# Loading and squaring the second row tile first, in a fixed order of the first norms, with norm weights on 97 rows

## The chip, the cores and the metric

The kernel runs on one core of a Trainium2 chip. A core has TensorE (PE, matrix multiply; its weight loads are listed as PEld), VectorE (DVE), ScalarE (ACT), GpSimd (POOL) and SyncE (SP), which run side by side, each through its own queue in order, and 16 DMA engines that serve all queues. The metric is the time of one execution on the device in microseconds. The kernel before took 877.15 us, the median of three runs (876.75, 877.15, 880.12).

## The reference, cut to what matters

The program is one encoder layer on 512 rows (tokens) of width 1024 in float32: an RMS norm, a product with `w_in`, two parallel mixers (a state-space scan and a gated chunk mixer), a gated merge, cross-attention to a memory of 256 rows, and a gated feed-forward part.

```python
def rms_norm(x, g):
    xf = x.astype(jnp.float32)
    y = xf * lax.rsqrt(jnp.mean(xf * xf, axis=-1, keepdims=True) + EPS)
    return (y * g.astype(jnp.float32)).astype(x.dtype)
...
        n = rms_norm(h, mix_norm_g[i])
        proj = n @ w_in[i]
        xa = proj[..., :OFF_U]
        zu = proj[..., OFF_U:OFF_V]
        zv = proj[..., OFF_V:OFF_GA]
```

Only the first norm and the first product, the first 512 columns of `zv`, are touched by the change.

## The kernel before

Rows are worked in four tiles of 128 (`xt[:, t, :]`, t = 0 to 3; x0 to x3 below). A float32 product is made of three products of a faster type: each operand is split into a high part, which ACT casts, and a low part, which DVE gets by subtraction (`split`, L85 and L86); `mm3` (L358) multiplies high by high, high by low and low by high. So each k tile of 128 costs three matmuls, and each weight block costs a cast and a subtraction before its first use.

Weights come in blocks of 512 KB in an order laid down in `plan`. A block is loaded by SP (`load_raw`, L137), split (`split_w`) and used (`next_w`); `raw`, `hi` and `lo` have three buffers each. The first product is a token product (`tokm`, L399): a bank of PSUM per row tile, four weight blocks of two k tiles each (w0 to w3), each used for the four row tiles. `tok_block` does one row tile with one or more blocks. One row tile with one block is six matmuls, the whole first product 96.

The start, before the first product, is in `first_rows` (L575) and the loop behind it (L598):

- Six idle matmuls (`idles`) go to PE, on a tile `idle` of the auxiliary PSUM pool (three buffers); the product banks are five.
- SP loads the norm's weights as one row (`g_row`), the first half of x0, w0, x1, w1, x2, w2, x3. ACT's queue loads the second half of x0. Two matmuls with a one-row operand (L579) spread `g_row` over 128 partitions into PSUM (`pg`).
- `row_sums` (L502) squares each half of a row tile on ACT with a running sum. `rms_factor` (L490) adds the two sums and scales them on DVE (L495, L496) and takes the power -0.5 on POOL (L497). Two DVE instructions scale the halves by that factor and by the norm's weights (L583 for x0, straight out of `pg`; L512 for the others, from the copy `g_mix`, made by ACT).
- `to_feat` (L514) transposes four 128x128 pieces on PE into an auxiliary bank (L520) and splits them into `xn_hi` and `xn_lo`.

All instructions are put in order, engine by engine, by a planner that simulates the program with its own costs. `in_order` pins an instruction behind the one traced just before it on its engine; while `pinned[0]` is true, `split` and `sum_sq` pin theirs. Behind the start, a side program (`s5_setup`, L620) prepares the scan: it loads small parameters, exponentiates the step sizes (L672, on ACT) and is spread between the products by `tick`.

Of the kernel before, what the change touches and what calls it, by code (L numbers as in the profile page):

```python
# [9 lines left out]
F32 = mybir.dt.float32  # L10
F32R = mybir.dt.float32r
AF = mybir.ActivationFunctionType
ALU = mybir.AluOpType
# [4 lines left out]
P = 128  # L18
D = 1024
T = 512  # L20
NT = T // P
KD = D // P
M = 256
NM = M // P
EPS = 1e-6
# [10 lines left out]
OFF_V = OFF_U + GW  # L36
# [16 lines left out]
def hybrid_layer_kernel(  # L53
# [8 lines left out]
    nc = tc.nc  # L62
    x, mem, out = x[0], mem[0], out[0]
    w_in, w_glu, w_proj_a, w_proj_b, w_out = w_in[0], s5_w_glu[0], w_proj_a[0], w_proj_b[0], w_out[0]
# [6 lines left out]
    np_ = ctx.enter_context(tc.tile_pool(name="norm", bufs=2))  # L71
# [5 lines left out]
    def bank(name):  # L77
        return pm.tile([P, 512], F32, tag="mm", name=name)

    def aux(name, shape=(P, 512)):  # L80
        return pa.tile(list(shape), F32, tag="aux", name=name)

    def split(dst_hi, dst_lo, src):

        hi = nc.scalar.copy(dst_hi, src)  # L85
        lo = nc.vector.tensor_tensor(dst_lo, src, dst_hi.bitcast(F32), ALU.subtract)  # L86
        if pinned[0]:
            in_order(hi)
            in_order(lo)


    pinned = [False]
    in_order = tc.keep_in_program_order
# [5 lines left out]
    plan, tiles = [], []  # L99
# [60 lines left out]
    stp = [None]  # L160
# [169 lines left out]
    def next_w(*key):  # L330
        i = used_w[0]
        used_w[0] += 1
        assert len(plan[i][0]) == len(key) and plan[i][0][1:] == key[1:] and plan[i][0][0] is key[0]
        for j in range(i, min(i + FAR + 1, len(plan))):
            begin(j, i)
            if j - 1 >= len(tiles) and j - 1 <= i + SPLITS:
                split_w(j - 1)
        for j in range(len(tiles), min(i + SPLITS + 1, len(plan))):
            split_w(j)
        tile_, tiles[i] = tiles[i], None  # L340
        return tile_
# [7 lines left out]
    def load_raw(j):  # L349
        begin(j, j)  # L350

    def split_w(j):
        tiles.append(plan[j][2]())
# [45 lines left out]
    def tokm(w, c0, act, nk, evac, ntok=NT, last=2, kpt=2, hooks={}, cut=None, t0=0):  # L399


        toks = range(t0, t0 + ntok)
        ps = {t: bank(f"pt{t - t0}") for t in toks}
        nw = nk // kpt
        held = []
        full = slice(0, 512)
        for wi in range(nw):
            hi, lo = next_w(w, wi * kpt, kpt, c0, 512)
            held.append((wi, hi, lo))
            if wi in hooks:  # L410
                hooks[wi]()
            if wi < nw - last:
                todo, held = held, []
                for t in toks:
                    end = cut is not None and t == ntok - 1 and wi == nw - last - 1
                    tok_block(ps[t], t, todo, act, kpt, full, wi == 0, end)
                    if end:
                        cut(None, ps[t])
                tick(1.3 * ntok)
        for t in toks:  # L420
            if cut is not None and t == ntok - 1:
                for i in range(2):
                    p = aux("pcut", (P, 256))
                    tok_block(p, t, held, act, kpt, slice(256 * i, 256 * i + 256), True, True)
                    cut(i, p)
            else:
                tok_block(ps[t], t, held, act, kpt, full, nw == last, True)
                evac(t, ps[t])
            tick(1.3 * len(held))

    def tok_block(ps, t, ws, act, kpt, cs, first, final):
        tsl = slice(t * P, (t + 1) * P)
        for i, (wi, hi, lo) in enumerate(ws):
            for k in range(kpt):
                kk = wi * kpt + k
                mm3(ps, (act[0](kk, tsl), act[1](kk, tsl)) if callable(act[0]) else
                    (act[0][:, kk, tsl], act[1][:, kk, tsl]),
                    (hi[:, k, cs], lo[:, k, cs]), first and i == k == 0,
                    final and i == len(ws) - 1 and k == kpt - 1)

    side = {"gen": None, "credit": 0.0, "rate": 0.0, "now": 0, "later": []}

# [47 lines left out]
    def rms_factor(ss, r=None):  # L490

        ms = np_.tile([P, 1], F32, tag="ms", name="ms", bufs=2)
        if r is None:
            r = np_.tile([P, 1], F32, tag="r", name="r", bufs=2)
        nc.vector.tensor_tensor(ms, ss[:, 0:1], ss[:, 1:2], ALU.add)  # L495
        nc.vector.tensor_scalar(ms, ms, 1.0 / D, EPS, ALU.mult, ALU.add)  # L496
        nc.gpsimd.tensor_tensor(r, ms, mhalf, ALU.pow)  # L497
        return r

    HALF = (slice(0, 512), slice(512, 1024))  # L500

    def row_sums(src):  # L502
        ss = np_.tile([P, 2], F32, tag="ss", name="ss", bufs=2)
        for i in range(2):
            sum_sq(ss[:, i:i + 1], src[:, HALF[i]])
        return ss

# [3 lines left out]
        for i in range(2):  # L511
            nc.vector.scalar_tensor_tensor(dst[:, HALF[i]], src[:, HALF[i]], r, g[:, HALF[i]], ALU.mult, ALU.mult)  # L512

    def to_feat(src, hi, lo, tsl, full=None, skip=None, part=(0, 1)):  # L514

        for q in part:
            ps = aux("ptr", (P, 4, P))
            for j in range(4):
                k = 4 * q + j
                nc.tensor.transpose(ps[:, j, :], src[:, k * P:(k + 1) * P], ident)  # L520
            if q != skip:
                split(hi[:, 4 * q:4 * q + 4, tsl], lo[:, 4 * q:4 * q + 4, tsl], ps)
            if full is not None:
                nc.scalar.copy(full[:, 4 * q:4 * q + 4, tsl], ps)
# [19 lines left out]
    def token_slot(name, place=NEAR):  # L544
        return tuple(slot(tag, (P, KD, T), F32R, name, place) for tag in "BC")
# [3 lines left out]
    s5p = s5.enter_context(tc.tile_pool(name="s5", bufs=1))  # L549


    idle = aux("idle", (P, P))

    def idles(n):
        for i in range(n):
            in_order(nc.tensor.matmul(idle, ones, ones, start=True, stop=True))
# [2 lines left out]
    warm = np_.tile([P, 1], F32, tag="ms", name="warm", bufs=2)  # L559
    nc.scalar.activation(warm, mhalf, AF.Square)  # L560


    g_mix = np_.tile([P, D], F32, tag="gain", name="g_mix", bufs=2)
    g_row = np_.tile([1, D], F32, tag="gain", name="g_row", bufs=2)
    nc.sync.dma_start(g_row, mix_norm_g)
    xt = slot("A", (P, NT, D), F32, "xt")
    nc.sync.dma_start(xt[:, 0, HALF[0]], x[0:P, HALF[0]])
    nc.scalar.dma_start(xt[:, 0, HALF[1]], x[0:P, HALF[1]])
    for t in range(1, NT):
        load_raw(t - 1)  # L570
        nc.sync.dma_start(xt[:, t, :], x[t * P:(t + 1) * P])
    xn_hi, xn_lo = token_slot("xn")
    xn = (xn_hi, xn_lo)

    def first_rows():  # L575

        pg = [aux("pg") for i in range(2)]
        for i in range(2):
            in_order(nc.tensor.matmul(pg[i], ones[0:1, :], g_row[:, HALF[i]], start=True, stop=True))  # L579
        r = rms_factor(row_sums(xt[:, 0, :]))  # L580
        in_order(nc.scalar.copy(g_mix[:, HALF[0]], pg[0]))
        for i in range(2):
            in_order(nc.vector.scalar_tensor_tensor(xt[:, 0, HALF[i]], xt[:, 0, HALF[i]], r, pg[i], ALU.mult, ALU.mult))  # L583
        raw = plan[0][3].pop("raw")
        hi = wp.tile([P, 2, 512], F32R, tag="hi", name="whi", bufs=3)
        lo = wp.tile([P, 2, 512], F32R, tag="lo", name="wlo", bufs=3)
        pinned[0] = True
        for q in range(2):
            split(hi[:, q, :], lo[:, q, :], raw[:, q, :])
            if q == 0:  # L590
                in_order(nc.scalar.copy(g_mix[:, HALF[1]], pg[1]))
            to_feat(xt[:, 0, :], xn_hi, xn_lo, slice(0, P), part=(q,))
        tiles.append((hi, lo))

    first_rows()
    split_w(1)
    ss = row_sums(xt[:, 1, :])
    for t in range(1, NT):  # L598
        rms_scale(xt[:, t, :], g_mix, xt[:, t, :], ss)
        if t == 1:  # L600
            ss = row_sums(xt[:, 2, :])
        to_feat(xt[:, t, :], xn_hi, xn_lo, slice(t * P, (t + 1) * P))
        if t == 1:
            ss3 = row_sums(xt[:, 3, :])
            pinned[0] = False
        if t == 2:
            ss = ss3

    ud = dp.tile([SW, Q, NCH], F32, name="ud")
    yd = [dp.tile([GO * C, Q, NCH], F32, name=f"yd{o}") for o in range(NO)]
# [4 lines left out]
    def s5_setup():  # L620
# [4 lines left out]
        def small():  # L625
            used[0] += 1
            return slab[:, used[0] - 1, :]

        ls = small()
        for d in range(2):  # L630
            nc.sync.dma_start(ls[64 * d:64 * d + 64, :], s5_log_step[0, d].partition_broadcast(64))
        lam = []
        lrows = s5p.tile([G, 2, 2, 64], F32, tag="etmp", name="lrows")
        for i, src in enumerate((s5_lam_re, s5_lam_im)):
# [33 lines left out]
        st["c"] = (cr, ci)  # L668


        stp, a, rho, th, n, sn, hs, cs = (small() for _ in range(8))
        A_.activation(stp, ls, AF.Exp)  # L672
        V.tensor_tensor(a, lr, stp, ALU.mult)
        A_.activation(rho, a, AF.Exp)
        V.tensor_tensor(th, li, stp, ALU.mult)
# [343 lines left out]
    def zv_evac(half):  # L1019
        def f(t, ps):  # L1020
            nc.scalar.activation(zt[:, t, half * 512:(half + 1) * 512], ps, AF.Gelu_apprx_tanh,
                                 accum_out=zsum[:, t, half:half + 1])
        return f
# [2 lines left out]
    wsr, wst = wsx[:, 0], wsx[:, 1]  # L1026
    side["gen"] = s5_program()
    side["rate"] = RATE
    tokm(w_in, OFF_V, xn, KD, zv_evac(0))

    u = s5p.tile([P, G, NCH], F32, tag="u", name="u")

# [503 lines left out]
    held = []  # L1536
# [324 lines left out]
```

## Time and profile before

| | us |
|---|---|
| median of three runs | 877.15 |
| profiled execution | 876.45 |
| its span, first to last instruction | 874.7 |
| PE busy | 862.7 (99%) |
| DVE busy | 660.7 (76%) |
| ACT busy | 464.3 (53%) |
| first product matmul starts | 9.64 |
| first matmul of the next product starts | 41.77 |

The span is shorter than the time by what lies before the first and after the last instruction. The page gives busy time by engine, the chain of work that ended last and the costliest groups; the timeline gives instructions in order of time with what ended the idle time before them. An arrow `out<-in` names the tile written and the tiles read.

### The profile page before, as it was taken

The numbers are of one execution on the slowest core, as the hardware profiler recorded it, in microseconds if no ns is written. First come the engines' busy times: TensorE is split into PE (matmuls) and PEld (weight loads), VectorE is DVE, ScalarE is ACT, GpSimd is POOL, SyncE is SP. The second block draws the span as 40 slices with busy tenths as digits, with TensorE's granted clock in tenths as the row PEclk, the third lists the DMA queues.
The fourth block names the chain that finished last, engine by engine and source line by source line (L and its number), as shares of the span: only waits on it lengthen the run. The fifth ranks groups of instructions, "written<-read, shape, count | busy, mean of one in ns | idle before, by whom it ended". The sixth has DMA issues, their size and how long they took to land.

```text
span 874.7 us, 14741 instructions
## 1 busy us (share of the span) xinstructions
PE 862.7 (99%) x5766; PEld 767.7 (88%) x5766; DVE 660.7 (76%) x1072; ACT 464.3 (53%) x693; POOL 85.1 (10%) x115
## 2 busy tenths in 40 slices
PE   9999999999999999999999999999999999999997
PEld 6788888888889988889899878999999999988875
DVE  6699885999846768568757746767877768899875
ACT  5644953244255543447546535545555555656664
POOL 1002201211020001100001001001111111000010
PEclk9999999999999999999999999999999999999999
DMA  8769565888663898735688655547899998366673
GB/s 254 198 191 291 112 174 147 194 228 202 157 196 95 275 319 236 255 95 168 196 244 247 157 135 154 145 144 174 214 243 229 209 234 218 97 191 206 193 230 106
DMA packets 116488, 169.56 MB, mean 194 GB/s; under 512 B 9265, under 2 KB 81473, under 8 KB 116290
## 3 DMA queue, kind: packets, MB, share of 16 engines
q1 hardware_dynamic: 96450, 140.59, 50.2%
q0 software_dynamic: 19680, 27.50, 20.1%
q8 instruction: 45, 0.74, 0.3%
q10 hardware_dynamic: 288, 0.52, 0.2%
q14 instruction: 25, 0.20, 0.1%
HBM read 159.71 MB, written 48.73 MB: 238 GB/s over the span
## 4 chain that ended last, share of the span: by engine, by line
PE 90%; DMA 4%; DVE 3%; ACT 2%; issue 1%; SPq 1%; DVEq 0%; ACTq 0%
PE pf L358 26%; PE pt L358 17%; PE px L1156 12%; PE pq L1156 6%; PE dx L358 5%; PE dq L358 3%; PE pv L1156 3%; PE qx L1156 2%; PE dv L358 2%; PE pz L890 2%; DMA e<-ed 1%; PE psc L358 1%; PE qq L1156 1%; PE ptr L520 1%; PE po L358 1%; DMA slab<-in_s_log_step_dram 1%
## 5 line engine op out<-in xcount | busy, mean ns | idle before, releaser
L85 ACT CAST whi<-wraw 128x1024 fp32r<-128x1024 f32 (+1 forms) x145 | 148.4, 1025 | 158.1 <-PE pf L358 54.8
L86 DVE TENSOR_TENSOR wlo<-wraw,whi 128x1024 fp32r<-128x1024 f32 (+1 forms) x145 | 172.0, 1189 | 66.8 <-ACT whi L85 66.1
L358 PE MATMUL pf<-xn,whi 128*128 128x512 f32 x448 | 140.3, 393 | 0.0
L358 PEld LDWEIGHTS pf<-xn,whi 128*128 128x128 f32 x448 | 83.7, 188 | 17.4 <-issue 0.4
L358 PE MATMUL pf<-xn,wlo 128*128 128x512 f32 x224 | 87.6, 392 | 0.0
L1156 PE MATMUL px<-fn,whi 128*128 128x256 f32 x480 | 83.3, 276 | 0.0
L1156 PEld LDWEIGHTS px<-fn,whi 128*128 128x128 f32 x480 | 72.5, 188 | 0.2
L86 DVE TENSOR_TENSOR wlo<-b,whi 128x1024 fp32r<-128x1024 f32 x40 | 48.9, 1223 | 27.4 <-ACT whi L85 27.4
L85 ACT CAST whi<-b 128x1024 fp32r<-128x1024 f32 x40 | 42.2, 1054 | 50.7 <-PE px L1156 27.8
L1156 PE MATMUL px<-fn,wlo 128*128 128x256 f32 x240 | 66.4, 277 | 0.0
L1156 PE MATMUL pq<-s,whi 128*128 128x256 f32 x320 | 55.0, 276 | 0.0
L358 PE MATMUL dx<-whi,s 128*128 128x512 f32 x166 | 52.2, 391 | 0.8 <-DVE h L1785 0.8
L86 DVE TENSOR_TENSOR wlo<-t,whi 128x1024 fp32r<-128x1024 f32 x30 | 36.8, 1225 | 19.5 <-ACT whi L85 19.5
L85 ACT CAST whi<-t 128x1024 fp32r<-128x1024 f32 x30 | 31.6, 1054 | 35.3 <-PE pv L1156 12.4
L358 PEld LDWEIGHTS pf<-xn,wlo 128*128 128x128 f32 x224 | 42.1, 188 | 8.8 <-issue 0.2
L1156 PEld LDWEIGHTS pq<-s,whi 128*128 128x128 f32 x320 | 48.2, 188 | 0.0
L1156 PEld LDWEIGHTS px<-fn,wlo 128*128 128x128 f32 x240 | 45.1, 188 | 0.0
L358 PE MATMUL pt<-whi,xn 128*128 128x512 f32 x128 | 44.2, 413 | 0.6 <-ACT xn L85 0.6
L1156 PE MATMUL pq<-s,wlo 128*128 128x256 f32 x160 | 44.2, 276 | 0.0
L358 PEld LDWEIGHTS dx<-whi,s 128*128 128x128 f32 x166 | 31.1, 188 | 7.8 <-issue 1.2
L358 PE MATMUL dx<-wlo,s 128*128 128x512 f32 x83 | 32.3, 391 | 0.0
L1156 PEld LDWEIGHTS pq<-s,wlo 128*128 128x128 f32 x160 | 30.1, 188 | 0.0
(454 smaller groups left out, 2195.0 us busy)
## 6 DMA issues: line engine op xcount, KB each, us to landing
wraw<-in_w_in_dram SPq DMA_DIRECT2D x36, 512.0 KB, 4.9
dsum<-in_w_down_dram SPq DMA_DIRECT2D x20, 512.0 KB, 6.2
wraw<-dsum SPq DMA_DIRECT2D x20, 512.0 KB, 3.9
b<-in_w_gate_dram SPq DMA_DIRECT2D x15, 512.0 KB, 5.2
b<-in_w_up_dram SPq DMA_DIRECT2D x15, 512.0 KB, 5.7
wraw<-in_w_down_dram SPq DMA_DIRECT2D x15, 512.0 KB, 4.7
dsum<-in_w_down_dram POOLq DMA_DIRECT2D x10, 512.0 KB, 7.7
dsum<-dsum POOLq DMA_DIRECT2D x10, 512.0 KB, 8.2
```

What stands on the lines that cost most here:

```text
L85: hi = nc.scalar.copy(dst_hi, src)
L86: lo = nc.vector.tensor_tensor(dst_lo, src, dst_hi.bitcast(F32), ALU.subtract)
L358: m = nc.tensor.matmul(ps, a[x], b[y], start=start and i == 0, stop=stop and i == 2, skip_group_check=free)
L520: nc.tensor.transpose(ps[:, j, :], src[:, k * P:(k + 1) * P], ident)
L890: nc.tensor.matmul(ps[:, g, :], wt[:, g, :], u[:, o * GO + g, :], start=True, stop=True)
L1156: nc.tensor.matmul(ps[:, j, :], a[x], b[y], start=start and j == k == i == 0, stop=k == 3 and i == 2, skip_group_check=True)
```

## The change

- SP's order of loads becomes `g_row`, first half of x0, x1, w0, w1, x2, w2, x3.
- `g_row` has 97 partitions: DVE clears rows 0 to 95, the weights are loaded into row 96, and the two spreading matmuls take 97 rows of ones and of `g_row`.
- The second half of x0 is squared before the first half.
- The whole of `first_rows` is pinned on PE, ACT and DVE. Both first row tiles are squared before anything of the first product. The second half of `g_mix` is copied by DVE, not by ACT. Three idle matmuls stand between the transposes of x0's first half and the first product. The product itself begins inside `first_rows`: the blocks (row tile, weight block) come as (0,0), (0,1), (1,0), (1,1), with the transposes and scalings of x0 and x1 in between. Six matmuls of a block are pinned too (`turn`).
- `tokm` is not used for the first product: row tiles 2 and 3 follow with w0 and w1, then all four with w2 and w3.
- The Exp of the step sizes is traced at the head of `s5_setup` and pinned on ACT.
- `idle` lies in a bank of the product pool.

```diff
-    def row_sums(src):
+    def row_sums(src, halves_=(0, 1)):
         ss = np_.tile([P, 2], F32, tag="ss", name="ss", bufs=2)
-        for i in range(2):
+        for i in halves_:
             sum_sq(ss[:, i:i + 1], src[:, HALF[i]])
...
-    idle = aux("idle", (P, P))
+    idle = bank("idle")[:, :P]
...
+    G_ROW = 96
     g_mix = np_.tile([P, D], F32, tag="gain", name="g_mix", bufs=2)
-    g_row = np_.tile([1, D], F32, tag="gain", name="g_row", bufs=2)
-    nc.sync.dma_start(g_row, mix_norm_g)
+    g_row = np_.tile([P, D], F32, tag="gain", name="g_row", bufs=2)
+    nc.vector.memset(g_row[0:G_ROW], 0.0)
+    nc.sync.dma_start(g_row[G_ROW:G_ROW + 1], mix_norm_g)
...
     for t in range(1, NT):
-        load_raw(t - 1)
         nc.sync.dma_start(xt[:, t, :], x[t * P:(t + 1) * P])
+        for i in ((0, 1), (2,), ())[t - 1]:
+            load_raw(i)
...
+    def row_feat(t, q):
+        to_feat(xt[:, t, :], xn_hi, xn_lo, slice(t * P, (t + 1) * P), part=(q,), turned=True)
+
+    def row_scale(t, i, r, g):
+        in_order(nc.vector.scalar_tensor_tensor(xt[:, t, HALF[i]], xt[:, t, HALF[i]], r, g, ALU.mult, ALU.mult))
+
     def first_rows():
-
         pg = [aux("pg") for i in range(2)]
         for i in range(2):
-            in_order(nc.tensor.matmul(pg[i], ones[0:1, :], g_row[:, HALF[i]], start=True, stop=True))
-        r = rms_factor(row_sums(xt[:, 0, :]))
+            in_order(nc.tensor.matmul(pg[i], ones[0:G_ROW + 1, :], g_row[0:G_ROW + 1, HALF[i]], start=True, stop=True))
+        pinned[0] = True
+        ss = row_sums(xt[:, 0, :], (1, 0))
+        r = rms_factor(ss)
         in_order(nc.scalar.copy(g_mix[:, HALF[0]], pg[0]))
         for i in range(2):
-            in_order(nc.vector.scalar_tensor_tensor(xt[:, 0, HALF[i]], xt[:, 0, HALF[i]], r, pg[i], ALU.mult, ALU.mult))
+            row_scale(0, i, r, pg[i])
+        in_order(nc.vector.tensor_copy(g_mix[:, HALF[1]], pg[1]))
+        r = rms_factor(row_sums(xt[:, 1, :]))
+        row_feat(0, 0)
+        idles(3)
         raw = plan[0][3].pop("raw")
         hi = wp.tile([P, 2, 512], F32R, tag="hi", name="whi", bufs=3)
         lo = wp.tile([P, 2, 512], F32R, tag="lo", name="wlo", bufs=3)
-        pinned[0] = True
-        for q in range(2):
-            split(hi[:, q, :], lo[:, q, :], raw[:, q, :])
-            if q == 0:
-                in_order(nc.scalar.copy(g_mix[:, HALF[1]], pg[1]))
-            to_feat(xt[:, 0, :], xn_hi, xn_lo, slice(0, P), part=(q,))
+        for k in range(2):
+            split(hi[:, k, :], lo[:, k, :], raw[:, k, :])
+            if k == 0:
+                row_scale(1, 0, r, g_mix[:, HALF[0]])
         tiles.append((hi, lo))
+        first_product(0, 0)
+        row_feat(1, 0)
+        split_w(1)
+        row_scale(1, 1, r, g_mix[:, HALF[1]])
+        first_product(0, 1)
+        ss = row_sums(xt[:, 2, :])
+        row_feat(0, 1)
+        first_product(1, 0)
+        first_product(1, 1)
+        row_feat(1, 1)
+        pinned[0] = False
+        return ss
...
+    def first_product(t, wi, turn=True):
+        tok_block(pt[t], t, [(wi,) + tiles[wi]], xn, 2, slice(0, 512), wi == 0, False, turn)
+
+    ss = first_rows()
+    for t in range(2, NT):
         rms_scale(xt[:, t, :], g_mix, xt[:, t, :], ss)
-        if t == 1:
-            ss = row_sums(xt[:, 2, :])
+        if t == 2:
+            ss = row_sums(xt[:, 3, :])
         to_feat(xt[:, t, :], xn_hi, xn_lo, slice(t * P, (t + 1) * P))
...
+        stp = small()
+        in_order(A_.activation(stp, ls, AF.Exp))
...
-    tokm(w_in, OFF_V, xn, KD, zv_evac(0))
+    evac = zv_evac(0)
+    for wi in range(2):
+        held = tiles[wi]
+        next_w(w_in, wi * 2, 2, OFF_V, 512)
+        tiles[wi] = held
+        for t in range(2, NT):
+            first_product(t, wi, False)
+        tiles[wi] = None
+        tick(5.2)
+    held = [(wi,) + next_w(w_in, wi * 2, 2, OFF_V, 512) for wi in (2, 3)]
+    for t in range(NT):
+        tok_block(pt[t], t, held, xn, 2, slice(0, 512), False, True)
+        evac(t, pt[t])
+        tick(2.6)
```

More of the change, by code (lines that the diff above doesn't have):

```diff
@@ L429, in tokm, with tok_block @@
             tick(1.3 * len(held))
-    def tok_block(ps, t, ws, act, kpt, cs, first, final):
+    def tok_block(ps, t, ws, act, kpt, cs, first, final, turn=False):
         tsl = slice(t * P, (t + 1) * P)
@@ L438, in tok_block @@
                     (hi[:, k, cs], lo[:, k, cs]), first and i == k == 0,
-                    final and i == len(ws) - 1 and k == kpt - 1)
+                    final and i == len(ws) - 1 and k == kpt - 1, turn=turn)
     side = {"gen": None, "credit": 0.0, "rate": 0.0, "now": 0, "later": []}
@@ L494, in rms_factor @@
             r = np_.tile([P, 1], F32, tag="r", name="r", bufs=2)
-        nc.vector.tensor_tensor(ms, ss[:, 0:1], ss[:, 1:2], ALU.add)
-        nc.vector.tensor_scalar(ms, ms, 1.0 / D, EPS, ALU.mult, ALU.add)
+        fixed = in_order if pinned[0] else lambda i: i
+        fixed(nc.vector.tensor_tensor(ms, ss[:, 0:1], ss[:, 1:2], ALU.add))
+        fixed(nc.vector.tensor_scalar(ms, ms, 1.0 / D, EPS, ALU.mult, ALU.add))
         nc.gpsimd.tensor_tensor(r, ms, mhalf, ALU.pow)
@@ L512, in rms_scale, with to_feat @@
             nc.vector.scalar_tensor_tensor(dst[:, HALF[i]], src[:, HALF[i]], r, g[:, HALF[i]], ALU.mult, ALU.mult)
-    def to_feat(src, hi, lo, tsl, full=None, skip=None, part=(0, 1)):
+    def to_feat(src, hi, lo, tsl, full=None, skip=None, part=(0, 1), turned=False):
         for q in part:
@@ L519, in to_feat @@
                 k = 4 * q + j
-                nc.tensor.transpose(ps[:, j, :], src[:, k * P:(k + 1) * P], ident)
+                m = nc.tensor.transpose(ps[:, j, :], src[:, k * P:(k + 1) * P], ident)
+                if turned:
+                    in_order(m)
             if q != skip:
@@ L586, in first_rows @@
         lo = wp.tile([P, 2, 512], F32R, tag="lo", name="wlo", bufs=3)
-        pinned[0] = True
-        for q in range(2):
-            split(hi[:, q, :], lo[:, q, :], raw[:, q, :])
-            if q == 0:
-                in_order(nc.scalar.copy(g_mix[:, HALF[1]], pg[1]))
-            to_feat(xt[:, 0, :], xn_hi, xn_lo, slice(0, P), part=(q,))
-        tiles.append((hi, lo))
[L595 to L598, printed above, removed]
+        for k in range(2):
+            split(hi[:, k, :], lo[:, k, :], raw[:, k, :])
+            if k == 0:
+                row_scale(1, 0, r, g_mix[:, HALF[0]])
+        tiles.append((hi, lo))
+        first_product(0, 0)
[10 more added lines that the diff above has]
+        return ss
+    pt = {t: bank(f"pt{t}") for t in range(NT)}
+    def first_product(t, wi, turn=True):
+        tok_block(pt[t], t, [(wi,) + tiles[wi]], xn, 2, slice(0, 512), wi == 0, False, turn)
+    ss = first_rows()
+    for t in range(2, NT):
         rms_scale(xt[:, t, :], g_mix, xt[:, t, :], ss)
-        if t == 1:
-            ss = row_sums(xt[:, 2, :])
+        if t == 2:
+            ss = row_sums(xt[:, 3, :])
         to_feat(xt[:, t, :], xn_hi, xn_lo, slice(t * P, (t + 1) * P))
[L603 to L607, printed above, removed]
     ud = dp.tile([SW, Q, NCH], F32, name="ud")
@@ L668, in s5_setup @@
         st["c"] = (cr, ci)
-        stp, a, rho, th, n, sn, hs, cs = (small() for _ in range(8))
-        A_.activation(stp, ls, AF.Exp)
+        a, rho, th, n, sn, hs, cs = (small() for _ in range(7))
         V.tensor_tensor(a, lr, stp, ALU.mult)
```

## The prediction

> **What bounds the kernel now.** I read the page's busy table first, then the chain that ended last, then the timeline of the first 42 us, because the diff touches nothing that runs later. The page:
>
> ```profile
> span 874.7 us, 14741 instructions
> ...
> PE 862.7 (99%) x5766; PEld 767.7 (88%) x5766; DVE 660.7 (76%) x1072; ACT 464.3 (53%) x693; POOL 85.1 (10%) x115
> ...
> PE 90%; DMA 4%; DVE 3%; ACT 2%; issue 1%; SPq 1%; DVEq 0%; ACTq 0%
> ```
>
> PE is busy for 99% of the span and carries 90% of the chain. Whatever the change does, the later 830 us are bound by PE, whose work there stays the same: an edit to the start moves the end by as much as it moves the moment at which PE has a given amount of work behind it. So I need the start, instruction by instruction (columns of the timeline: start, length, engine, line, operation, and in brackets the idle time before it with what ended it).
>
> ```profile
> 1.06 2.93 PE L556 MATMUL idle<-ones 128*128 128x128 f32 x12 [1.06 <-DVE mhalf L481]
> 1.56 0.43 SPq L137 DMA_DIRECT2D wraw<-in_w_in_dram  x1
> 2.03 0.47 SPq L571 DMA_DIRECT2D xt<-in_x_dram  x1
> 3.92 3.78 PE L579 MATMUL pg<-g_row,ones 1*128 1x512 f32 x4
> 4.50 0.63 ACT L486 ACTIVATE sq<-xt 128x512 f32<-128x512 f32 x1 [1.84 <-DMA xt<-in_x_dram]
> 5.58 1.20 SPq L631 DMA_DIRECT2D slab<-in_s_log_step_dram  x2
> 5.65 0.19 ACT L486 ACTIVATION_READ_ACCUMULATOR sq<-xt 128x1 f32 x1
> 5.87 0.16 DVE L495 TENSOR_TENSOR ms<-ss 128x1 f32<-128x1 f32 x1 [3.68 <-ACT sq L486]
> 6.30 0.57 POOL L497 TENSOR_TENSOR r<-ms,mhalf 128x1 f32<-128x1 f32 x1 [4.53 <-DVE ms L496]
> 6.90 1.58 DVE L583 SCALAR_TENSOR_TENSOR xt<-xt,r,pg 128x512 f32<-128x512 f32 x2 [0.68 <-POOL r L497]
> 7.58 0.62 ACT L85 CAST whi<-wraw 128x512 fp32r<-128x512 f32 x1 [0.97 <-DMA wraw<-in_w_in_dram]
> 7.79 1.94 PE L520 MATMUL ptr<-ident,xt 128*128 128x128 f32 x8
> 8.40 0.68 DVE L86 TENSOR_TENSOR wlo<-wraw,whi 128x512 fp32r<-128x512 f32 x1
> 9.64 0.80 PE L358 MATMUL pt<-whi,xn 128*128 128x512 f32 x1
> 10.24 0.63 PE L358 MATMUL pt<-wlo,xn 128*128 128x512 f32 x1
> 10.47 1.07 ACT L85 CAST whi<-wraw 128x1024 fp32r<-128x1024 f32 x1
> 10.66 1.06 PE L358 MATMUL pt<-whi,xn 128*128 128x512 f32 x2
> 11.58 1.22 DVE L86 TENSOR_TENSOR wlo<-wraw,whi 128x1024 fp32r<-128x1024 f32 x1
> 13.33 0.63 PE L358 MATMUL pt<-whi,xn 128*128 128x512 f32 x2
> 13.79 0.40 PE L358 MATMUL pt<-wlo,xn 128*128 128x512 f32 x1
> 14.62 1.38 PE L520 MATMUL ptr<-ident,xt 128*128 128x128 f32 x8
> 15.83 0.23 ACT L672 ACTIVATE slab<-slab 128x32 f32<-128x32 f32 x1 [0.68 <-DMA slab<-in_s_log_step_dram]
> 16.59 0.50 PE L358 MATMUL pt<-whi,xn 128*128 128x512 f32 x1 [0.58 <-ACT xn L85]
> 20.35 0.62 PE L358 MATMUL pt<-whi,xn 128*128 128x512 f32 x2
> 20.80 0.39 PE L358 MATMUL pt<-wlo,xn 128*128 128x512 f32 x1
> 21.03 0.62 PE L358 MATMUL pt<-whi,xn 128*128 128x512 f32 x2
> 21.94 1.47 PE L520 MATMUL ptr<-ident,xt 128*128 128x128 f32 x12
> 28.25 0.19 DVE L673 TENSOR_TENSOR slab<-slab 128x32 f32<-128x32 f32 x1
> 41.77 0.62 PE L358 MATMUL pf<-xn,whi 128*128 128x512 f32 x2
> ```
>
> See two things. At 10.24 to 10.66 one product matmul takes 0.42 us from start to start; from 20.35 to 21.03 three take 0.68, or 0.227 each. At 13.33 to 13.79 two take 0.46: PE ran at half speed until about 13. And PE has a hole around 16: the Exp of L672 stood in front of the x cast on ACT and waited 0.68 us for a small load.
>
> ```profile
> 9.62:21.93 12.31, 10.35 (x36) 1.00 1.02 259
> 21.93:41.76 19.83, 15.60 (x61) 1.00 0.72 200
> ```
>
> These rows (stretches of time, PE on tile pt alone: length, busy, number of matmuls; one falls into both) are my yardstick: by 21.94 PE has 36 product matmuls and 16 transposes behind it. 36 x 0.227 = 8.2 us, and the 8 transposes of row tile 1 at about 0.11 us (12 in 1.47 with the last one's tail) another 0.9. Of 12.3 us some 3.2 were lost to the slow clock and to holes. This is all that a better start can win from 9.64 on. After 21.94 PE is busy throughout.
>
> **The change, part by part.** *Loads.* x1 and w0 change places on SP's queue, one issue slot of about 0.45 us (1.56 to 2.03); nothing else on SP or on ACT's queue moves. In the trace the first half-megabyte behind x0 (w0) was there at 7.58, when the cast that waited for it started, and x1, issued second at 2.03, landed 6.8 us later; x0's second half, on ACT's queue from its start at about 0.75, took 3.1 (columns: size, us from issue to landing):
>
> ```profile
> xt<-in_x_dram SPq DMA_DIRECT2D x1, 512.0 KB, 6.8
> xt<-in_x_dram ACTq DMA_DIRECT2D x1, 256.0 KB, 3.1
> ```
>
> So I give the first place's 7.5 to x1 and the second's 8.85 to w0; w1, x2, w2 and x3 keep their places. g_row goes to row 96 while DVE clears rows 0 to 95. The memset is priced by that of `ones`: 128 columns cost 165 ns, so 1,024 cost at most 8 times that, 1.3 us:
>
> ```profile
> L479 DVE MEMSET ones<- 128x128 f32 x1 | 0.2, 165 | 0.8 <-PEq L1847 0.8
> L955 DVE COPY yn<-py 128x512 f32<-128x512 f32 x4 | 2.8, 692 | 10.3 <-PE pyt L961 10.3
> ```
>
> DVE is idle then (its 3.68 us before 5.87), so I take nothing for it. If g_row's load waited for the memset, SP's queue behind it would slip from 0.75 to about 2.4 us, by some 1.6; that is the upper end.
>
> *Gain matmuls and clock.* The two fp32 gain matmuls have 512 columns before and after, so their work is the same; only the rows change, 1 to 97. No row here shows 97. What rows show: PE was busy without a break from 1.06 to 9.6 and was still at half speed at 10.24; of that, 3.92 to 7.7 were one-row matmuls. The full-height products from 9.64 on had it at full speed some 3.5 to 4 us later. Nearest to 97 rows is 128, so I take it that they count, and that PE is at full speed from somewhere between 4.5 and 8 us. [...]
>
> *First norms.* The half that ACT's queue loads is squared first, so ACT starts at about 3.9 and has both halves by 5.25, not 5.84. The same steps follow: sum and scale on DVE, the power on POOL (0.57), r at 6.3; the first scaling 6.3 to 7.05, the second by 7.8. The copy of the gains' second half goes from ACT to DVE: 0.69 us by the L955 row, so DVE is free at 8.4 to 9.0. ACT copies the first half and then stands waiting for x1: its two squares take 7.55 to 8.9 (1.34 for the pair, 4.50 to 5.84). r of row tile 1 is there at 9.9.
>
> *The fixed order, and what it costs.* On ACT the cast of x0's first transposes (eight took 1.94 at half speed, so four are ready at 8.8, or 7.6 at full speed) is queued behind the squares of x1: 8.9 to 9.5. Then w0's two halves, 9.5 to 10.1 and to 10.75. On DVE the order is x0's low part to 10.2, w0's first low half to 10.9, the scaling of x1 (0.75) to 11.65, w0's second low half to 12.3. So PE, with three idle matmuls covered (six took 2.93 at half speed, so three are 1.5 at most, from 7.6 or 8.8 on, while ACT squares x1 and casts; without that cover they cost their 0.7 to 1.5), begins its first product at 10.15, but its fifth matmul needs the second low half: block (0,0) ends at 12.8 and not before. Only then come x1's four transposes, to 13.3; only then, on ACT, their cast, 13.45 to 14.05; only behind that w1's cast (1.07) to 15.1; w1's low part on DVE (1.22) to 16.35. Block (0,1) gets its second matmul at 16.35 and ends at 17.5. From there PE is dense: four transposes to 17.95, two blocks of six (2.7 us) to 20.7, four transposes to 21.1.
>
> At 21.1 PE then has 24 products and 16 transposes. The yardstick has 36: 12 x 0.227 = 2.7 us more, so the new kernel reaches the same state at 23.8, against 21.94: 1.9 us late.
>
> *Steps at no cost.* Exp leaves the middle of ACT's queue and stands behind the last x cast, near 25 us by my sum: its result is first used at 28.25, and the 0.68 us wait goes; the sum above holds it already, since the new wait on w1's cast is later still. The squares of x2 and w2's split fall in ACT's time after 15.1, while PE works from 16.35 on. The idle tile takes a product bank instead of an auxiliary one; four token banks and it fill the five. The new order over tokens and weights in the first product moves 96 matmuls about but adds none. The small gain left out: with PE later, x2 and x3 are less likely to keep it waiting; I take 0.2 us.
>
> Sum: +1.9 - 0.2 = +1.7. The profiled execution took 876.45 (span 874.7 and 1.75 around it), 0.7 below the median of 877.15. So 876.45 + 1.7 = 878.1, 1.0 above the median, or 0.1%. A measurement of this kernel can hardly tell 0.5% (4.4 us) from no change.
>
> **Rivals.** *The clock stays low (slower).* If 97 rows do not count, products cost 0.42 until PE has been dense for 3.5 us. By the same chain the first block ends at 13.2, w1's low part at 17.15, block (0,1) at 19.3; the clock rises at about 20.5, the 24th product and the transposes end at 23.3: 2.2 us more, 880.3. If the clock rises only at 24, the twelve products and eight transposes from 19.3 on cost up to 2.6 more, 882. It decides against 881.5 when dense work must last about 4.5 us from 17.15. For it: PE is half empty from 8 to 16. Against it: the clock held through the thin stretch at 14.65 to 16.6 and fell only after the last matmul, and PE's longest hole in my forecast is 1.8 us:
>
> ```profile
> 868.23 0.28 PE L358 MATMUL pcut<-whi,s 128*128 128x256 f32 x1
> 872.00:874.70 2.70, 0.00 (x0) 0.75 0.46 175
> ```
>
> Three quarters of the clock on the mean over the last 2.7 us: it fell about 5 us after the last matmul. Chance 0.22, over half of that still within 0.5%.
>
> *The order is kinder than I count (slightly faster).* If x1 lands at 6.5 and DVE gets w0's second low half before PE needs it, PE is dense from about 12.3: four products left of the first twelve plus the next twelve with their transposes end at 18.2, against 19.2 for the same state before (21.94 - 2.7): 1.0 us gained, 875.4. For it: no row shows x1 in the first place; against it: each engine's queue in the diff keeps its order, so w1's cast cannot pass x1's. Chance 0.25. A gain over 0.5% needs 872.8; the 3.2 us lost in the yardstick stretch are the ceiling (873.2), and w0 lands later, so 0.02.
>
> *SP's queue waits for the memset.* +1.6 on the whole chain: 879.7. Against it: the two loads of L631 write two row ranges of one tile, and the second was issued by 6.78, long before anything of them had landed (near 15.8, where Exp's wait ended). Chance 0.08.
>
> **How the numbers follow.** Forecast 0.45, low clock 0.22, kinder order 0.25, memset 0.08. Range: down to 874.8, the 875.4 of the kinder order with 0.6 for the early landing of x1; up to 881.6, between the two ends of the low clock. Within 0.5% (872.8 to 881.5): 0.87; slower 0.11; faster 0.02.
>
> **What would show it.** After's timeline: ACT's squares of x1 waiting for its load until about 7.5; transposes of x0 at about 0.11 us each if the clock is up by 8; w1's cast starting behind x1's cast near 14; a PE hole before it, and the product blocks dense from 16.4; no DMA wait of ACT before Exp. The first feature product (L358, pf, at 41.77 before) should start near 43.5. Wrong would be: w1 cast before 12, PE dense by 13, or product matmuls at 0.42 after 16.

## The result and the profile after

The changed kernel takes 881.5 us (median of six runs, 880.98 to 882.23), the kernel before 876.95 in the six runs beside it: a ratio of 1.0050, 95% interval 1.0037 to 1.0064. In a second comparison (E5 below) it took 880.3 against 877.2, ratio 1.0037 (1.0023 to 1.0051). It is slower, by 0.4 to 0.5%.

The page of the kernel after:

```profile
span 879.6 us, 14755 instructions
...
PE 861.7 (98%) x5772; PEld 768.2 (87%) x5772; DVE 662.0 (75%) x1074; ACT 463.7 (53%) x692; POOL 86.1 (10%) x115
...
PEclk8999999999999999999999999999999999999999
```

The span is 4.9 us longer and PE is busy 1.0 us less: PE waits more, and most of that in the first slice. The clock row reads 8 there and 9 on the page before, but the rows do not compare directly: the page counts the clock as full up to its first recorded change, which came at 4.12 us here and only at 13.19 before. The timeline of the start of the kernel after (start, length, engine, line, operation, idle time before it and what ended it) against the rows of the prediction:

```profile
0.75 0.35 SPq L569 DMA_DIRECT2D g_row<-in_mix_norm_g_dram  x1
1.18 0.91 DVE L568 MEMSET g_row<- 96x1024 f32 x1 [0.16 <-issue]
3.39 0.63 ACT L486 ACTIVATE sq<-xt 128x512 f32<-128x512 f32 x1 [0.73 <-DMA xt<-in_x_dram]
7.62 0.63 ACT L486 ACTIVATE sq<-xt 128x512 f32<-128x512 f32 x1 [2.02 <-DMA xt<-in_x_dram]
8.86 0.56 ACT L85 CAST xn<-ptr 128x512 fp32r<-128x512 f32 x1
9.99 0.51 PE L358 MATMUL pt<-whi,xn 128*128 128x512 f32 x1 [1.94 <-ACT whi L85]
13.08 1.05 PE L521 MATMUL ptr<-ident,xt 128*128 128x128 f32 x4
14.17 0.58 ACT L85 CAST xn<-ptr 128x512 fp32r<-128x512 f32 x1 [3.71 <-PE ptr L521]
14.65 1.05 ACT L85 CAST whi<-wraw 128x1024 fp32r<-128x1024 f32 x1
15.76 0.50 PE L358 MATMUL pt<-whi,xn 128*128 128x512 f32 x1 [1.62 <-ACT whi L85]
17.02 0.50 PE L358 MATMUL pt<-wlo,xn 128*128 128x512 f32 x1 [0.77 <-DVE wlo L86]
17.77 0.23 ACT L652 ACTIVATE slab<-slab 128x32 f32<-128x32 f32 x1
18.69 1.06 PE L521 MATMUL ptr<-ident,xt 128*128 128x128 f32 x4
23.05 1.03 PE L521 MATMUL ptr<-ident,xt 128*128 128x128 f32 x8
45.77 0.62 PE L358 MATMUL pf<-xn,whi 128*128 128x512 f32 x2
```

ACT stands idle for 3.71 us before the cast of x1 at 14.17, although w1 has been loaded since about 10.2 (issued near 2.5, landed 7.7 us later); PE then has no work from 14.1 to 15.76 and next to none to 17.02. The first feature product starts at 45.77 instead of 41.77. The windows of PE alone in the kernel after, in steps of the 3.41 us that lie between two of its changes of clock, 10.95 and 14.36 (stretch, length, busy, number of matmuls, granted clock):

```profile
4.12:7.53 3.41, 2.53 (x11) 1.00 0.84 273
7.53:10.95 3.42, 1.18 (x7) 1.00 1.04 407
10.95:14.36 3.41, 3.19 (x9) 0.50 0.97 308
14.36:17.77 3.41, 1.25 (x4) 1.00 1.02 161
17.77:21.19 3.42, 3.42 (x11) 0.50 1.05 223
```

The clock is up from 4.12, falls at 10.95, rises at 14.36, falls at 17.77 just as the work becomes dense, and is up from 21.19 to 877.93, near the end of the span. In the 3.42 us before the first fall PE was busy for 1.18 us, in the 3.41 before the second for 1.25. So 4.0 us are lost by 45.8. A further 1.0 comes where PE waits for small loads of the scan's outputs. The waits of PE between 240 and 280 us (us in total, times, longest), first after, then before:

```profile
PE py L966 <- DMA e<-ed: 1.8, 1, 1.8
PE py L966 <- DMA tt<-kd: 1.0, 3, 0.4
```

```profile
PE py L946 <- DMA e<-ed: 1.2, 1, 1.2
PE py L946 <- DMA tt<-kd: 0.6, 2, 0.3
```

### The profile page after: what moved, and what is told of

Its sections match the earlier page's. It is cut to its first block, busy times and chain, and to the rows that moved or that the text cites. A ratio compares the mean times of both kernels' runs of the same rounds, so it can differ in the third digit from the quotient of the medians.

```text
span 879.6 us, 14755 instructions
## 1 busy us (share of the span) xinstructions
PE 861.7 (98%) x5772; PEld 768.2 (87%) x5772; DVE 662.0 (75%) x1074; ACT 463.7 (53%) x692; POOL 86.1 (10%) x115
## 4 chain that ended last, share of the span: by engine, by line
PE 91%; DMA 4%; DVE 2%; ACT 1%; issue 1%; SPq 0%; ACTq 0%; DVEq 0%
PE pf L358 26%; PE pt L358 18%; PE px L1189 12%; PE pq L1189 6%; PE dx L358 5%; PE dq L358 3%; PE pv L1189 3%; PE qx L1189 2%; PE dv L358 2%; PE pz L910 2%; DMA e<-ed 1%; PE ptr L521 1%; PE bx L1189 1%; PE psc L358 1%; PE qq L1189 1%; PE po L358 1%
## 5 line engine op out<-in xcount | busy, mean ns | idle before, releaser
L358 PEld LDWEIGHTS pf<-xn,whi 128*128 128x128 f32 x448 | 83.7, 188 | 17.3 <-issue 0.4
L358 PEld LDWEIGHTS pt<-whi,xn 128*128 128x128 f32 x128 | 24.5, 196 | 9.1 <-ACT whi L85 4.2
```

What stands on the lines that cost most here:

```text
L358: m = nc.tensor.matmul(ps, a[x], b[y], start=start and i == 0, stop=stop and i == 2, skip_group_check=free)
```

## The experiments

Two theories stood after the result. A: the fixed order starves PE (the cast of w1 is pinned on ACT behind a cast of x1 that itself waits for PE), and the thin stretches then bring the clock down. B: only the order counts, the clock is without effect. A third, C: the first weights come too late, behind x1 on the load queue. "Feature product" below is the start of the first `pf` matmul in the profile, 41.77 before and 45.77 after; times are medians, with the ratio to the kernel before in the same comparison (877.5 for E1 to E4, 877.2 for E5 to E8, 876.5 for E9 and E10).

### E1: the changed kernel with one-row gain matmuls

```diff
-    g_row = np_.tile([P, D], F32, tag="gain", name="g_row", bufs=2)
-    nc.vector.memset(g_row[0:G_ROW], 0.0)
-    nc.sync.dma_start(g_row[G_ROW:G_ROW + 1], mix_norm_g)
+    g_row = np_.tile([1, D], F32, tag="gain", name="g_row", bufs=2)
+    nc.sync.dma_start(g_row, mix_norm_g)
...
-            in_order(nc.tensor.matmul(pg[i], ones[0:G_ROW + 1, :], g_row[0:G_ROW + 1, HALF[i]], start=True, stop=True))
+            in_order(nc.tensor.matmul(pg[i], ones[0:1, :], g_row[:, HALF[i]], start=True, stop=True))
```

> The changed kernel with its gain matmuls on one row again, as before the change. In the changed kernel's profile the clock was full from 4.1 to 11 us, half to 14.4, full to 17.8, half to 21.2. Theory A (the fixed order leaves PE thin and the clock falls with it; 97 rows do count): without the 97 rows the clock stays half until PE is dense, from 17.0 on, so the block that now begins at 17.0 runs at 0.43 us a matmul throughout and the first feature product starts at 46 to 48 us instead of 45.8; time 881.5 to 883.5. Theory B (only the order of ACT and DVE counts, the clock does not): 45.8 and 881.5 as they are.

Measured: 880.1 us, ratio 1.0026 (1.0008 to 1.0045); feature product at 45.66. Windows of PE:

```profile
13.60:17.02 3.42, 1.04 (x5) 1.00 0.80 138
17.02:20.43 3.41, 3.41 (x11) 0.50 0.84 195
```

Nothing is lost against the changed kernel (881.5 and, in E5, 880.3), which contradicts the number that A gave. The clock rose only at 13.60 here, PE was busy for 1.04 of the next 3.42 us, and the clock was down from 17.02 to 20.43, close to the 17.77 to 21.19 of the changed kernel. In this order the 97 rows buy nothing that the times show: what they win is gone again before PE can use it. The number is the one that B gave; E2 shows that B is not the reason.

### E2: the holes filled with idle matmuls

```diff
-        idles(3)
+        idles(11)
...
         row_feat(1, 0)
+        idles(9)
         split_w(1)
```

> The changed kernel with eight more idle matmuls in the hole before the first product (11 in place of 3) and nine more behind the first transposes of row tile 1, in the hole before the second block. Theory A (thin stretches of PE drop the clock): the clock stays full from about 4 us on, the matmuls from 17.0 to 21 take 0.23 instead of 0.43, the feature product starts at 43.6 to 44.2 instead of 45.8, time 879.5. Theory B (the clock does not count): 45.8 or later, 881.5 or up to 0.5 more for the idle matmuls.

Measured: 878.2 us, ratio 1.0001 (0.9983 to 1.0019). The window that follows the second hole, and the feature product:

```profile
13.93:17.35 3.42, 2.78 (x19) 1.00 0.66 129
17.35:20.76 3.41, 3.41 (x19) 1.00 0.89 224
```

```profile
43.29 0.61 PE L358 MATMUL pf<-xn,whi 128*128 128x512 f32 x2
```

The order is unchanged and PE does 17 more idle matmuls, yet the feature product comes 2.5 us earlier than in the first profile (1.4 earlier than in that of E5) and the time falls by 2.1 us against 880.3 of E5 (3.3 against the first 881.5). The clock does not fall after its rise at 7.11 (1.00 in every stretch to 27.59). B is out. What is left against the profile before, 43.29 - 41.77 = 1.5 us, is the order's price, less what the earlier clock gives back (up from 7.11 here, from 13.19 there). It is read from one profile of each; the times of E2 and of the kernel before are not told apart.

### E3: w1 split ahead of x1's first cast

```diff
-        row_feat(1, 0)
         split_w(1)
+        row_feat(1, 0)
```

> The changed kernel with the split of the second weight block (w1) put ahead of the transposes and the cast of row tile 1's first half. Theory A (w1's cast is stuck on ACT behind the cast of x1, which waits for PE): the cast of w1 starts at about 10.5 instead of 14.65, its low part is there by 13.2, PE is dense from about 12 and the clock does not fall a second time; the feature product starts at 41.7 to 42.5 instead of 45.8, time 877.5 to 878.5. Rival C (the late first weights, behind x1 on the queue, set the start): at most 1 us gained, time 880.5 to 881.5.

Measured: 876.2 us, ratio 0.9986 (0.9967 to 1.0006). ACT, then PE in the timeline:

```profile
10.15 1.05 ACT L85 CAST whi<-wraw 128x1024 fp32r<-128x1024 f32 x1 [0.19 <-DMA wraw<-in_w_in_dram]
12.96 1.05 ACT L85 CAST whi<-wraw 128x1024 fp32r<-128x1024 f32 x1 [1.76 <-DMA wraw<-in_w_in_dram]
13.91 0.58 ACT L85 CAST xn<-ptr 128x512 fp32r<-128x512 f32 x1
```

```profile
12.41 0.48 PE L358 MATMUL pt<-whi,xn 128*128 128x512 f32 x1
15.92 0.74 PE L358 MATMUL pt<-whi,xn 128*128 128x512 f32 x2 [0.64 <-DVE xn L86]
41.35 0.62 PE L358 MATMUL pf<-xn,whi 128*128 128x512 f32 x2
```

One pair of lines exchanged takes the whole loss back, more than A expected (877.5 to 878.5): w1 is cast at 10.15, block (0,1) starts at 12.41 instead of 15.76, the clock stays up without added matmuls after its rise at 5.69 (1.00 to 29.58), and the feature product is 4.4 us earlier. The load order is the changed one, so C does not explain the loss. Every other part of the change is still in place too (the split first product, the copy on DVE, the bank of the idle tile), so none of them carries it.

### E4: the kernel before with the 97 rows alone

```diff
-    g_row = np_.tile([1, D], F32, tag="gain", name="g_row", bufs=2)
-    nc.sync.dma_start(g_row, mix_norm_g)
+    G_ROW = 96
+    g_row = np_.tile([P, D], F32, tag="gain", name="g_row", bufs=2)
+    nc.vector.memset(g_row[0:G_ROW], 0.0)
+    nc.sync.dma_start(g_row[G_ROW:G_ROW + 1], mix_norm_g)
...
-            in_order(nc.tensor.matmul(pg[i], ones[0:1, :], g_row[:, HALF[i]], start=True, stop=True))
+            in_order(nc.tensor.matmul(pg[i], ones[0:G_ROW + 1, :], g_row[0:G_ROW + 1, HALF[i]], start=True, stop=True))
```

> The kernel before with the 97-row gain matmuls alone. Theory A: full clock from between 4 and 8 us; the first six products take 0.23 each, but the second weight block's low part still comes at 12.86 and the cast of row tile 1 still waits for the Exp, so the profile's feature product moves by 0 to 0.5 us from 41.8; executions in which the clock rises late gain more: median 0.5 to 1.5 below the kernel before, spread narrower than its 875.4 to 880.1. Unless the clock falls again in the thin stretches at 8 to 10 or 14.7 to 16.6: then up to 1 us slower. Theory B: no change.

Measured: 876.3 us against 877.5, ratio 0.9986 (0.9967 to 1.0006), not told from no change. The profiled execution, at 880.56 the slowest of its twelve, had the exception that the expectation named:

```profile
4.52:7.93 3.41, 1.83 (x7) 1.00 0.86 303
7.93:11.34 3.41, 3.08 (x11) 0.50 1.04 411
14.76:18.17 3.41, 1.38 (x9) 1.00 0.37 75
18.17:21.58 3.41, 3.15 (x7) 0.50 0.70 173
```

ACT waited 1.3 us for the small load of the Exp here (0.68 in the first profile), the hole around 16 became longer, the clock fell at 18.17, and the feature product came at 45.06. It had risen at 4.52 and fallen once before, at 7.93, with the 97 rows in place. So the order of before lost to the clock too in this execution.

### E5: the changed kernel again

No edit; it puts the changed kernel into one comparison with E6 to E8 and gives a second profile.

> The changed kernel unaltered, to stand in one comparison with the others and to give a second profile. What is open: in its first profile 4.0 us of the loss stood at the first feature product (45.8 against 41.8) and 1.0 more came at 262 to 269 us, where PE waited 2.8 us for small loads instead of 1.8. If that is chance, this profile has 1.4 to 2.0 us of such waits; if the change causes it, 2.8 again. Theory A (thin PE drops the clock, in windows that lie differently in each execution): the clock rows lie elsewhere, with at least one stretch of 3.4 us at half speed between 7 and 22 us; feature product at 44 to 46.5, median 880.5 to 882.

Measured: 880.3 us (twelve runs, 879.4 to 883.2), feature product at 44.65. Windows, the second matmul of block (0,1), and waits:

```profile
12.99:16.40 3.41, 1.04 (x3) 1.00 0.88 157
16.40:19.82 3.42, 3.42 (x11) 0.50 0.76 185
```

```profile
15.87 0.50 PE L358 MATMUL pt<-wlo,xn 128*128 128x512 f32 x1 [0.76 <-DVE wlo L86]
```

```profile
PE py L966 <- DMA e<-ed: 1.4, 1, 1.4
PE py L966 <- DMA tt<-kd: 0.6, 2, 0.4
```

The first fall of the clock is absent here and the second came 1.4 us earlier (16.40 against 17.77). With the clock up until 16.4, that matmul starts 1.15 us earlier than in the first profile (0.23 of it by an earlier first product). The late waits are 2.0 us, near the 1.8 of before, so the long wait of the first profile is not a fixed part of the change. The time from the feature product to the end is 833.8 us in both profiles all the same, against 832.9 before; over the twelve profiles it goes from 831.7 to 834.1, with 832.9 in E6 and 833.9 in E8. Whether the change adds anything behind the feature product stays open.

### E6: the loads in the order of before

```diff
     for t in range(1, NT):
+        load_raw(t - 1)
         nc.sync.dma_start(xt[:, t, :], x[t * P:(t + 1) * P])
-        for i in ((0, 1), (2,), ())[t - 1]:
-            load_raw(i)
```

> The changed kernel with the loads in the order of before (w0 ahead of x1, as w0, x1, w1, x2, w2, x3), all else as changed. Theory A (everything on ACT is queued behind the squares of x1): x1 comes 1.3 us later, so its squares end at 10.2 instead of 8.8, the first product starts at 11.3 instead of 10.0 and the feature product 0.5 to 1.5 later than in the changed kernel beside it, time 0.5 to 1.5 more. Rival C (the late w0 is what costs): the first product starts earlier and the time falls by about 1 us.

Measured: 882.3 us, ratio 1.0056 (1.0035 to 1.0077); feature product at 47.70. ACT and PE:

```profile
9.04 0.63 ACT L486 ACTIVATE sq<-xt 128x512 f32<-128x512 f32 x1 [2.71 <-DMA xt<-in_x_dram]
```

```profile
11.41 0.51 PE L358 MATMUL pt<-whi,xn 128*128 128x512 f32 x1 [2.86 <-ACT whi L85]
```

The first product starts 1.4 us later although its weights come first. In this fixed order, with the squares of x1 at the head of ACT, loading x1 first is right; C is out. The loss is larger than the 0.5 to 1.5 expected: in this profile the clock was down from 12.70 to 22.94, so a part of it is the clock's.

### E7: the kernel before with the Exp traced early and pinned

```diff
         ls = small()
...
+        stp = small()
+        in_order(A_.activation(stp, ls, AF.Exp))
...
-        A_.activation(stp, ls, AF.Exp)
```

> The kernel before with only the Exp of the step sizes traced early and pinned behind the last cast of x. Expected by both theories: ACT does not wait at 15.2 for the small load, the cast of row tile 1 starts 0.5 to 0.9 earlier than 16.0, PE's hole before 16.6 shrinks by as much, and with less of a hole the clock falls less often; feature product at 40.9 to 41.4 where the clock stays up, median 0.5 to 1.5 below the kernel before. If the wait only moves to another place: no change.

Measured: 878.1 us, ratio 1.0002 (0.9988 to 1.0016). This did not do what it was made for. On ACT:

```profile
18.55 0.23 ACT L633 ACTIVATE slab<-slab 128x32 f32<-128x32 f32 x1 [2.28 <-DMA slab<-in_s_log_step_dram]
```

The pin holds the Exp behind the cast traced just before it, which is one of w2, not behind the last cast of x. It still stood ahead of x1's cast and waited 2.28 us, since the load came later in this execution. The clock fell at 7.45, after 3.41 us in which PE was busy for 1.90, all of it with one-row matmuls, and was up again at 14.27; the feature product came at 44.50. What an Exp truly behind the casts would give the kernel before was not tried.

### E8: w1 first, and seven idle matmuls before the first product

```diff
-        idles(3)
+        idles(7)
...
-        row_feat(1, 0)
         split_w(1)
+        row_feat(1, 0)
```

> The changed kernel with w1's split ahead of row tile 1's first cast, and seven idle matmuls instead of three before the first product. Theory A: the feature product at 41.0 to 41.6, no stretch at half speed after the first rise in any window from 7 us on, median 875.5 to 876.2 against 876.2 of the version with w1 first alone, and a narrower spread (that one had 874.2 to 879.2). Theory B (the clock does not count): the same as w1 first alone.

Measured: 876.4 us, ratio 0.9990 (0.9978 to 1.0002); feature product at 41.34, no fall of the clock (1.00 from 6.65 to 27.13), eleven of twelve runs between 875.3 and 877.6. That is no gain against E3, and just above the 875.5 to 876.2 expected. ACT shows what both versions still lose:

```profile
13.24 1.05 ACT L85 CAST whi<-wraw 128x1024 fp32r<-128x1024 f32 x1 [1.94 <-DMA wraw<-in_w_in_dram]
14.19 0.58 ACT L85 CAST xn<-ptr 128x512 fp32r<-128x512 f32 x1
```

The planner put w2's cast ahead of x1's, where ACT waited for w2's load.

### E9: w1 first, with one-row gain matmuls

The edits of E1 and E3 together.

> The changed kernel with w1's split ahead of row tile 1's first cast, and the gain matmuls on one row. Theory A (97 rows do raise the clock early, and it is worth something once the order lets PE use it): without them the clock rises only after PE has been dense, at 13 to 17 us, so the twelve products from 9.5 to 14 take 0.43 each; feature product at 42.5 to 44 against 41.4 with 97 rows, median 877 to 879 against 876.2. Theory B (rows do not matter once the order is right): 41.4 and 876.2.

Measured: 876.8 us, ratio 1.0000 (0.9989 to 1.0012); feature product at 42.46, 1.1 us behind E3. The windows:

```profile
1.06:4.47 3.41, 3.41 (x13) 1.00 0.76 239
4.47:7.88 3.41, 2.58 (x12) 1.00 0.87 290
7.88:11.30 3.42, 1.88 (x6) 0.50 1.05 413
```

The clock column shows 1.00 until the first change is recorded; the first row is at half speed: its twelve idle matmuls took 2.93 us, and in E2 at full speed 22 took 2.62. The clock rose at 4.47, when the idle matmuls had run from 1.06 to 3.99, and fell again at 7.88, after 3.41 us in which PE was busy for 2.58, most of it with one-row matmuls. In the changed kernel PE was busy for 2.53 us from 4.12 to 7.53, 1.72 of them in 97-row matmuls, and the clock was still at 1.00 behind it. The feature product moved as A said, the time did not: 877 to 879 was expected. The 0.6 us between the medians of E3 and E9 are from two comparisons and inside their intervals.

### E10: w1 first, seven idle matmuls, and w2 pinned behind x1's cast

```diff
-        idles(3)
+        idles(7)
...
-        row_feat(1, 0)
         split_w(1)
+        row_feat(1, 0)
         row_scale(1, 1, r, g_mix[:, HALF[1]])
+        split_w(2)
```

> The changed kernel with w1's split ahead of row tile 1's first cast, seven idle matmuls before the first product, and w2's split pinned behind that cast. In the version with w1 first the planner had put w2's cast in front of the cast of row tile 1, where ACT waited 1.9 us for w2's load (13.24) while the transposes lay ready since about 12.7, and PE lost 0.25 and 0.64 us at 14.8 and 16.2. Theory A: the cast of row tile 1 starts at 12.6 to 13, both holes go, feature product at 40.2 to 40.9, median 875 to 875.8, 0.1 to 0.2% under the kernel before. If the holes only move to the wait for w2: 41.3 and 876.3, as without the pin.

Measured: 874.8 us (873.7 to 876.9) against 876.5, ratio 0.9976 (0.9966 to 0.9987): faster than both kernels. ACT and PE:

```profile
13.28 0.59 ACT L85 CAST xn<-ptr 128x512 fp32r<-128x512 f32 x1 [1.87 <-PE ptr L521]
13.76 1.05 ACT L85 CAST whi<-wraw 128x1024 fp32r<-128x1024 f32 x1
```

```profile
40.48 0.62 PE L358 MATMUL pf<-xn,whi 128*128 128x512 f32 x2
```

From 12.1 on PE has no hole, and the feature product is 1.3 us earlier than in the kernel before, 5.3 earlier than in the changed one. Three small edits inside the fixed order decide between 0.5% slower and 0.24% faster. The interval of E10 just overlaps that of E8; that the pin of w2 made the step rests on the two ACT timelines.

## Why the prediction was right or wrong

**Direction and size.** The forecast was 878.1, 1.0 us above the median; measured were 3.1 to 4.6 above it. It ended within the range only at its upper edge, and the ratio lies at the edge of the half per cent that the forecast called hard to tell from no change; the interval, 1.0037 to 1.0064, does tell it. A small loss was expected for a reason that proved right, and a second loss of the same size was left out. The upper end of the range came from a rival with another mechanism, so that the time lies inside it is in part luck.

**The fixed order: right.** The steps came nearly where the sum had them: squares of x1 at 7.62 (7.55), cast of x0 at 8.86 (8.9), first product at 9.99 (10.15), cast of w1 at 14.65 (14.05), the second matmul of block (0,1) at 17.02 (16.35). In E5, where the clock held longer, the second matmul of block (0,1) started at 15.87, ahead of the forecast. E2, the same order with the clock held up, has its feature product at 43.29; the forecast had named 43.5. E3 shows that the link named in the working, w1's cast behind x1's on ACT, carries the loss.

**The clock: the step that failed.** The forecast took it that PE is at full speed from 4.5 to 8 us on and stays there ("the clock held through the thin stretch at 14.65 to 16.6"). The first half held: it rose at 4.12. That rise does not tell whether the 97 rows had a part in it: the idle matmuls had run from 1.06 to 3.99, and E7 and E9 rose at 4.04 and 4.47 with one row. In E2 the 97-row matmuls ran from 3.78 to 7.32 and the clock rose at 7.11; in E1 the one-row matmuls ran from 3.92 to 7.70 and it rose at 13.60. That 97 rows count like 128 was the author's estimate, and this one pair of profiles agrees with it. The second half did not hold: the clock fell twice. The holes at 8.05 to 9.99 and 14.1 to 15.76 were in the working, the longest was called 1.8 us, and they were compared with the one long pause at the end of the kernel, as if only a full pause counted. In the kernel before PE was busy for 2.73 of the 3.41 us from 13.19 to 16.60, and the clock stayed up; ahead of the two falls in the changed kernel it was busy for 1.18 and 1.25:

```profile
13.19:16.60 3.41, 2.73 (x15) 1.00 0.98 188
```

By the forecast the 24th product and the 16th transpose were done at 21.1; PE reached its eight transposes, four of them of x1, at 23.05 and finished x1's near 23.5, 2.4 us late: 0.7 by which the chain was late at 17.02, and 1.7 from the half speed between 17.77 and 21.19. The 0.7 is the clock's as well, by the comparison with E5: its first fall slowed block (0,0) and the transposes of x1 between 10.95 and 14.36.

**The rivals.** "The clock stays low" gave 880.3 to 882 and the time fell there, but by another course: the clock was up from 4.12 and fell at 10.95 and 17.77. The kinder order did not come, and is what E3 and E10 made of it. Its sum is off: from 12.3, sixteen products and twelve transposes at the forecast's own 0.227 and 0.11 us end near 17.3, not 18.2, so it should have been priced near 874.5; E10 took 874.8. The memset rival is out: `g_row`'s load was issued at 0.75 and the memset ran from 1.18 to 2.09 beside it.

**Smaller steps.** The first squares began at 3.39, not 3.9, which gained nothing because ACT then waited 2.02 us for x1. The Exp was said to stand behind the last cast of x, near 25 us; it stood at 17.77, behind w2's cast. In the changed kernel it did not wait there, but in E9 and E7 an Exp so pinned did. The load order was priced right, and undoing it in this order (E6) costs about 2 us (882.3 against 880.3), the clock's part included.

## What to carry to other kernels

When an order is fixed by hand, follow each engine's queue for an instruction that is ready but stands behind one that waits for the engine it should feed: here a weight cast behind an activation cast that waited for TensorE, worth 4.4 us at the feature product by the move of one line. Price a hole in TensorE's work twice, once for the hole and once for a fall of the clock behind it: in the changed kernel 1.62 us of idle time ahead of 15.76, and by estimate 1.7 us, half of the 3.42 at half speed from 17.77 to 21.19. Idle matmuls in the hole (E2) tell the two apart. Where an order is pinned, look at what the planner slips in between and pin that as well if it waits (E8 against E10).

## What the runs showed of the hardware

In the first 26 us of the twelve profiles the clock fell from 1.00 to 0.50 nine times. PE's busy time just before each fall, and how long half speed lasted:

| run | before the fall, us | PE busy, us | at 0.50, us |
|---|---|---|---|
| changed kernel | 7.53 to 10.95 | 1.18 | 10.95 to 14.36 |
| changed kernel | 14.36 to 17.77 | 1.25 | 17.77 to 21.19 |
| E1 | 13.60 to 17.02 | 1.04 | 17.02 to 20.43 |
| E4 | 4.52 to 7.93 | 1.83 | 7.93 to 11.34 |
| E4 | 14.76 to 18.17 | 1.38 | 18.17 to 21.58 |
| E5 | 12.99 to 16.40 | 1.04 | 16.40 to 19.82 |
| E6 | 9.29 to 12.70 | 0.99 | 12.70 to 22.94 |
| E7 | 4.04 to 7.45 | 1.90, one-row matmuls | 7.45 to 14.27 |
| E9 | 4.47 to 7.88 | 2.58, mostly one-row matmuls | 7.88 to 14.71 |

In E7 PE was busy for 1.80 us from 17.69 to 21.10, in E5 for 2.01 from 6.17 to 9.58, and the clock was at 1.00 behind both. The longest pause of PE that reached into one of the nine was 2.86 us, in E6, up to 11.41. These are single executions of this kernel's mix of products, transposes and idle matmuls; no bound for other work is shown.
